# Hyena stages of a three-branch encoder: more tiles read ahead, another share of the merge, two vector steps on ScalarE

## Chip, core and metric

One NeuronCore of one Trainium2 chip runs the whole program. The metric is the device time of one execution in microseconds (us). Engines are named as the profile names them: PE (TensorE matmul), PEld (its weight load), DVE (VectorE), ACT (ScalarE), POOL (GpSimd), SP (SyncE, whose queue issues nearly all transfers).

## What is computed

An encoder layer runs on a prompt of 512 rows and a sample of 2048 rows, 1024 columns wide. A normalised row is projected by `w_in` (6672 columns) to three head groups: mLSTM (4 heads), retention (4 heads) and Hyena (512 channels). Their gated results are joined to 1536 columns, projected back by `w_out`, added to the input and normalised again.

```python
def hyena_branch(hy_in, hy_z, conv_w, conv_b, spec, skip):
    u = centred_conv3(hy_in, conv_w, conv_b)
    v, x1, x2 = u[..., :HY_WIDTH], u[..., HY_WIDTH:2*HY_WIDTH], u[..., 2*HY_WIDTH:]
    z = x1 * long_conv(v, spec[:, 0], skip[0])
    z = x2 * long_conv(z, spec[:, 1], skip[1])
    return z * silu(hy_z)
```

`long_conv` is a product in the frequency domain. Its filters come from a small network with two sines, `sin(freq * (x @ w + b))`, whose hidden values are multiplied by `w3` and a decaying window.

## The kernel before, in words

All matmuls with `w_in` are split in fp16 high and low parts, three products for each. `proj_T` (line 539, L544) gives transposed results, four groups of 6 matmuls of 512 columns; `proj_N` (line 549, L554) gives row-wise ones. The rows stand in five blocks of 512, block 0 the prompt.

The stages follow each other so:

- `front` (line 238): norm and transposition of the rows, the first third of Hyena's input with its 3-tap convolution (`hyena_cols`, `conv`, L811 and L813), the gates (`hyena_gate`), the filter network (`filter_mlp`, `sin`, L562 to L568), and the first set of filters.
- the merge (line 232): one stream is Hyena's Fourier work, the other the rest of Hyena's projections (`projections`) and then all of retention. The Hyena stream is `stage_a0` (L921: transform over n1 of the first third, from `X` to `Sg`), `freq(0)` (L948, L983: transform over n2, product with the filter, transform back to `Z`), `inv_a(0)` (L1028: back over n1, product with x1, and forward again by `stage_a`), `freq(1)`, and `inv_a(1)` (L1028, product with x2 at L1029, with the gate at L1033 on POOL, store to `ymix` at L1036).
- `mlstm`, then `final` (the product with `w_out`).

A stage over n1 takes 20 tiles (L, j): 4 of the prompt, 16 of the sample. In `inv_a(1)` a tile loads two `hb` buffers of `Z` (L890, 256 KB each), one of `X` and one of the gate `hyg` in two halves each (L790, 128 KB a half), and stores one in two halves (L1036): eight transfers. All of them, and those of the other stream, are issued in order on SP. There are 18 `hb` buffers.

The order of the work is planned when the program is built. Generators yield a cost in microseconds of PE work; `lag(cost, lag)` (line 172) adds the time before which the stream is not to be taken again. `merge` (line 177) takes, of the streams that are due, the one with the smallest share of its total done, cost so far divided by the number given with it: `275 * W3` = 283.25 for Hyena and 848 for the other. If no stream is due, the planned time jumps to the next due one. The framework (`schedule_with_timeline_sim=True`) then orders the instructions of each engine by its own estimate of what is ready, with the planned order as priority; so an instruction can pass an earlier one.

Two waits of the planner matter at the start of the merge. `filters()` in `projections` (line 290) begins with `lag(0.0, FH)`, 8 us. A Hyena projection of group 1 or 2 stops after its first 24 matmuls (`while grp and grp - 1 not in self.scaled`, line 828) until the filters of the group before are summed.

The end of the merge is the last block of the last retention head (`RtHead.second`, `output`, lines 1673 to 1709), which has no next block to be merged with. Its lags are R1 = 2.5, R2 = 2.0, R3 = 1.5, four times R4 = 0.6, and LN = 1.5, around 0.86 + 0.43 + 4 x 0.43 us of PE cost and 0.1.

Of the kernel before, what the change touches and what calls it, by code (L numbers as in the profile page):

```python
# [14 lines left out]
AF = mybir.ActivationFunctionType  # L15
ALU = mybir.AluOpType
# [14 lines left out]
MAGIC = 12582912.0  # L31
# [7 lines left out]
LF, LA, LI, LT, W1, W2, W3, LN, LM = 2.7, 1.0, 4.2, 1.6, 0.8, 1.08, 1.03, 1.5, 3.5  # L39
# [4 lines left out]
def geo(L):  # L44
    N = 2 * L
    N1 = N // 64
    V = N1 // 2
    return dict(N=N, N1=N1, K1=N1 // 2, V=V, GF=128 // N1, GS=128 // V, NTF=N // 128, NTS=L // 128)
# [105 lines left out]
class Trunk:  # L154
# [62 lines left out]
    def run(self):  # L217
        tc = self.tc
        with ExitStack() as ctx:
            self.psum = ctx.enter_context(tc.tile_pool(name="psum", bufs=8, space=PSUM))  # L220
            self.dram = ctx.enter_context(tc.tile_pool(name="dram", bufs=1, space=DRAM))
            self.cp = ctx.enter_context(tc.tile_pool(name="cp", bufs=1))
            self.setup()
            with ExitStack() as c1:
                self.hp = c1.enter_context(tc.tile_pool(name="hp", bufs=1))
                self.wp = c1.enter_context(tc.tile_pool(name="wp", bufs=2))
                self.hT = [[self.T(self.hp, [128, 8, 512], "h", F16, bufs=10) for i in range(2)] for b in range(5)]
                self.filter_pool = ExitStack()
                self.drain(self.front())
                with tc.tile_pool(name="hy", bufs=2, side="right") as self.hy:  # L230
                    self.load_ai()
                    self.drain(self.merge((self.chain(self.stage_a0(), self.freq(0), self.inv_a(0), self.freq(1), self.inv_a(1)), 275 * W3),
                                          (self.chain(self.projections(), self.retention()), 848)))
                self.drain(self.mlstm())
                with tc.tile_pool(name="fin", bufs=2, **TW) as self.fin:
                    self.final()
# [322 lines left out]
    def sin(self, pool, out_list, x, p):  # L559
        nc = self.nc  # L560
        k = self.T(pool, [128, 512], "sink")
        nc.vector.tensor_scalar(k[:p], x, 1.0 / (2 * math.pi), MAGIC, op0=ALU.mult, op1=ALU.add)  # L562
        nc.vector.tensor_scalar(k[:p], k[:p], MAGIC, None, op0=ALU.subtract)
        nc.vector.scalar_tensor_tensor(x, k[:p], -PI_C1, x, op0=ALU.mult, op1=ALU.add)
        nc.vector.scalar_tensor_tensor(x, k[:p], -PI_C2, x, op0=ALU.mult, op1=ALU.add)
        nc.vector.tensor_scalar(x, x, PI_MAX, -PI_MAX, op0=ALU.min, op1=ALU.max)
        for o, i in out_list:
            nc.scalar.activation(o, i, AF.Sin)  # L568
# [22 lines left out]
    def mlp_setup(self):  # L591
        nc, I, pm = self.nc, self.I, self.pm
        w1 = self.T(pm, [33, 64], "w1", bufs=1)
        w2 = self.T(pm, [64, 2, 64], "w2", bufs=1)
        pv = self.T(pm, [128, 3], "pv", bufs=1)
        nc.sync.dma_start(w1, I['hy_w1'][0])
        for i in range(2):
            nc.sync.dma_start(w2[:, i], I['hy_w2'][0])
            for j, nmv in enumerate(('hy_b1', 'hy_b2', 'hy_freq')):
                nc.sync.dma_start(pv[i * 64:(i + 1) * 64, j:j + 1], I[nmv].rearrange("o k -> k o"))  # L600
        self.fm = (w1, w2, pv)
        self.hid = [self.T(self.dram, [128, 512], f"hid{i}") for i in range(10)]

    def filter_blocks(self):
# [201 lines left out]
                    nc.gpsimd.tensor_copy(us[nb][:, 513 - end:514 - end], u[:, own:own + 1])  # L806
        return us, put

    def conv(self, d, u, w, bias):
        nc = self.nc  # L810
        nc.vector.tensor_scalar(d, u[:, 0:512], w(0), bias, op0=ALU.mult, op1=ALU.add)  # L811
        for t in (1, 2):
            nc.vector.scalar_tensor_tensor(d, u[:, t:t + 512], w(t), d, op0=ALU.mult, op1=ALU.add)  # L813

    def hyena_cols(self, grp, cp, cis, w):

        nc, hc = self.nc, self.hyc
        cv = {}
        halo = {ci: self.halo_blocks(hc, range(5), f"u{cis.index(ci)}") for ci in cis}

        def step(b):
            for ci in cis:
                us, put = halo[ci]
                c = grp * 4 + 2 * cp + ci
                ps = self.ps()
                yield from self.proj_T(ps, w, ci * 128, b)
                put(b, ps, w[2])
                while grp and grp - 1 not in self.scaled:
                    yield self.lag(0.0, 1.0)
                for d in (x for x in range(5) if (x == b and b in (0, 4)) or (x == b - 1 and b > 1)):  # L830
                    L = LP if d == 0 else LS
                    if d < 2:
                        cv[ci, L] = self.T(hc, [128, L], f"cv{L}", bufs=len(cis))
                    s, o = self.sw[L], d * 512 - SEQ0[L]
                    self.conv(cv[ci, L][:, o:o + 512], us[d], lambda t: s[:, t, c:c + 1], s[:, 3, c:c + 1])
                yield 1.28

        def out(L):
            nt = geo(L)['NTS']
            for ci in cis:  # L840
                cb = 2 * cp + ci
                for j0 in range(0, nt, 4):
                    ps = self.ps()
                    for jj in range(4):
                        j = j0 + jj
                        nc.tensor.transpose(ps[:, jj * 128:(jj + 1) * 128], cv[ci, L][:, j:L:nt], self.ident)  # L846
                    xs = self.T(hc, [128, 4, 128], "xs", bufs=3)
                    nc.scalar.activation(xs, ps.rearrange("p (j c) -> p j c", j=4), AF.Copy)
                    nc.sync.dma_start(self.X[grp][L][j0:j0 + 4, :, cb * 128:(cb + 1) * 128].rearrange("j p c -> p j c"), xs)
                    yield 0.43  # L850
        return step, out

    def hyena_proj(self, grp, *after):
# [42 lines left out]
    def stage_a0(self):  # L896
        seq = [(L, j) for L in (LP, LS) for j in range(geo(L)['NTS'])]
        st = {}

        def load(i):  # L900
            L, j = seq[i]
            st[i] = self.hx(0, L, j)

        n = len(seq)
        load(0)
        load(1)
        for i in range(n + 1):
            if i:
                L, j = seq[i - 1]
                self.stage_a(L, 0, j, st.pop(i - 1))  # L910
            if i + 2 < n:
                load(i + 2)
            yield self.lag(0.86, 1.5)

    def stage_a(self, L, o, j, t):
        nc = self.nc
# [92 lines left out]
    def inv_a(self, o):  # L1009
        nc = self.nc  # L1010
        seq = [(L, j) for L in ((LS, LP), (LP, LS))[o] for j in range(geo(L)['NTS'])]
        zs, xs, st = {}, {}, {}

        def load(i):
            L, j = seq[i]
            zs[i] = [self.hb(self.Z[L, o][:, geo(L)['NTS'] * h + j::2 * geo(L)['NTS'], :]) for h in range(2)]

        def load_x(i):
            L, j = seq[i]
            g = self.in_halves(self.half_rows(self.hyg, L, j)) if o == 1 else None  # L1020
            xs[i] = self.hx(o + 1, L, j), g

        def mid(i):
            L, j = seq[i]
            z, (x, g) = zs.pop(i), xs.pop(i)
            ps = self.ps()
            for h in range(2):
                nc.tensor.matmul(ps[64 * h:64 * h + 64], self.ai[L][:, 128:192], z[h], start=True, stop=True)  # L1028
            nc.vector.tensor_tensor(out=x, in0=x, in1=ps, op=ALU.mult)  # L1029
            if o == 0:  # L1030
                st[i] = x
            else:
                nc.gpsimd.tensor_tensor(out=g, in0=g, in1=x, op=ALU.mult)  # L1033
                rows = self.half_rows(self.ymix[:, 1024:1536], L, j)
                for h in range(2):
                    nc.sync.dma_start(rows[h], g[64 * h:64 * h + 64])  # L1036

        def back(i):
            L, j = seq[i]
            self.stage_a(L, 1, j, st.pop(i))  # L1040

        n = len(seq)
        load(0)
        yield self.lag(0.0, 5.0)
        for i in range(-1, n + 1):
            if o == 0 and i >= 1:
                back(i - 1)
            if 0 <= i < n:
                mid(i)
            if i + 1 < n:  # L1050
                load_x(i + 1)
            if i + 2 < n:
                load(i + 2)
            yield self.lag(1.71 if o == 0 else 0.86, LI)

    def gates(self):
        nc, I, tc = self.nc, self.I, self.tc
# [678 lines left out]
```

## Time and profile before

| | us |
|---|---|
| median of 3 runs | 2651.07 |
| the runs | 2650.94 to 2654.84 |
| the profiled execution, its own time | 2648.68 |
| its span, first to last instruction | 2646.9 |
| mean granted clock of TensorE, share of full speed | 0.988 |

The span is what the views of the trace divide. The profiled execution's own time is 1.8 us longer than its span, and 2.4 us below the median of the runs. "Idle before" names what an engine waited for just before an instruction. A wait for several things is put down to the one that came last.

### The profile page before, as it was taken

The page shows a single profiled execution, that of the slowest core. Times are in us where ns is not written, and L with a number is a line of the kernel's source. Part 1 is how long each engine was busy: PE and PEld are TensorE (multiplying, and loading weights), DVE is VectorE, ACT ScalarE, POOL GpSimd, SP SyncE. Part 2 cuts the span into 40 slices and gives each one's busy share as a digit, 9 for nine tenths or more (in the row PEclk, how much of TensorE's full clock was granted, in tenths as well). Part 3 has the DMA queues.
Part 4 walks back from the last instruction along what each step waited for, and adds up shares of the span by engine and source line. Part 5 has one row for each costly group of instructions (what it writes and reads, how often), then busy time and mean ns, then how long its engine had stood idle before and what let it go on. Part 6 is the DMA issues. An engine that isn't in the chain of part 4 may idle for free.

```text
span 2646.9 us, 45607 instructions
## 1 busy us (share of the span) xinstructions
PE 2557.2 (97%) x17830; PEld 1770.2 (67%) x17830; DVE 1338.3 (51%) x3070; ACT 1053.7 (40%) x2030; POOL 493.9 (19%) x647
## 2 busy tenths in 40 slices
PE   7999979999999999999999979999999999899998
PEld 5565543444446777777777747787887777788887
DVE  6875635665554434545444444565556645522222
ACT  6455646442233333423333323555445545411111
POOL 0103312331011122322232341111111111100000
PEclk9999989999999999999999989999999999999999
DMA  6233377564454665434333782222121322322331
GB/s 207 84 99 108 98 220 252 167 187 127 126 160 128 207 198 160 126 100 132 116 104 97 226 228 65 52 66 61 37 64 42 89 73 59 133 102 95 111 104 48
DMA packets 238049, 321.30 MB, mean 121 GB/s; under 512 B 22755, under 2 KB 125947, under 8 KB 237833
## 3 DMA queue, kind: packets, MB, share of 16 engines
q1 hardware_dynamic: 237752, 318.11, 39.8%
q8 instruction: 141, 2.31, 0.4%
q14 instruction: 76, 0.61, 0.1%
q0 software_dynamic: 80, 0.26, 0.0%
HBM read 205.41 MB, written 112.89 MB: 120 GB/s over the span
## 4 chain that ended last, share of the span: by engine, by line
PE 78%; DMA 6%; ACT 4%; DVE 4%; issue 1%; SPq 1%; POOL 1%; DVEq 0%; POOLq 0%; ACTq 0%
PE ps L554 27%; PE ps L544 13%; PE ps L1287 13%; PE ps L948 6%; DMA rb<-rowd 3%; PE ps L983 3%; PE ps L1028 2%; PE ps L921 1%; PE ps L1639 1%; DMA wraw<-in_w_in 1%; PE ps L693 1%; PE ps L1438 1%; PE ps L1275 1%; PE ps L1698 1%; PE ps L846 1%
## 5 line engine op out<-in xcount | busy, mean ns | idle before, releaser
L554 PE MATMUL ps<-whi,h 128*128 128x256 f16 (+2 forms) x6080 | 913.7, 256 | 0.0
L554 PEld LDWEIGHTS <-h 128*128 128x128 f16 x9120 | 776.0, 98 | 150.0 <-issue 69.5
L554 PE MATMUL ps<-wlo,h 128*128 128x256 f16 (+2 forms) x3040 | 734.6, 256 | 0.0
L544 PE MATMUL ps<-h,whi 128*128 128x512 f16 x1600 | 484.9, 383 | 4.0 <-ACT whi L526 4.0
L544 PE MATMUL ps<-h,wlo 128*128 128x512 f16 x800 | 305.0, 381 | 0.0
L544 PEld LDWEIGHTS <-whi 128*128 128x128 f16 x1600 | 151.1, 99 | 212.8 <-issue 63.0
L1287 PE MATMUL ps<-h,yh 128*128 128x512 f32 x760 | 210.6, 396 | 1.6 <-ACT yh L369 1.6
L948 PE MATMUL ps<-hb,cB 128*64 128x512 f32 x640 | 165.9, 605 | 0.2 <-DMA hb<-F 0.2
L1287 PEld LDWEIGHTS ps<-h,yh 128*128 128x128 f32 x760 | 141.6, 188 | 33.7 <-ACT yh L369 1.9
L668 POOL TENSOR_TENSOR acc<-acc,win 128x512 f32<-128x512 f32 x80 | 107.2, 1340 | 201.4 <-ACT win L667 196.2
L544 PEld LDWEIGHTS <-wlo 128*128 128x128 f16 x800 | 78.7, 98 | 94.7 <-issue 4.9
L1618 POOL TENSOR_TENSOR m<-raw,tb 128x256 f32<-128x256 f32 x80 | 72.3, 904 | 336.2 <-ACT raw L1615 273.2
L1287 PE MATMUL ps<-h,yl 128*128 128x512 f32 x380 | 120.9, 395 | 0.0
L1615 ACT ACTIVATE raw<-ps,winv 128x256 f32<-128x256 f32 x80 | 37.8, 473 | 167.5 <-PE ps L554 98.9
L662 DVE TENSOR_TENSOR f<-ps,win 128x512 f32<-128x512 f32 x80 | 55.0, 688 | 88.7 <-PE ps L378 66.1
L813 DVE SCALAR_TENSOR_TENSOR cv<-u,sw,cv 128x512 f32<-128x512 f32 x120 | 98.1, 838 | 1.1
L527 DVE SCALAR_TENSOR_TENSOR wlo<-wraw,wsc,whi 128x512 f16<-128x512 f32 (+2 forms) x116 | 82.6, 749 | 22.8 <-ACT whi L526 21.6
L1637 ACT ACTIVATE vw<-va,rtv 128x128 f32<-128x128 f32 x144 | 51.9, 398 | 100.4 <-PE ps L1639 100.0
L948 PEld LDWEIGHTS ps<-hb,cB 128*64 128x64 f32 x640 | 41.5, 136 | 73.2 <-issue 60.6
L348 DVE TENSOR_REDUCE wam<-wraw 128x1 f32<-128x2048 f32 (+2 forms) x29 | 60.0, 2069 | 60.0 <-DMA wraw<-in_w_in 60.0
L1343 DVE TENSOR_TENSOR xt<-xt,ps 128x512 f32<-128x512 f32 x40 | 25.8, 684 | 126.9 <-PE ps L1287 126.9
L971 POOL TENSOR_TENSOR hb<-hb,hb 128x512 f32<-128x512 f32 x40 | 50.9, 1273 | 185.5 <-DVE hb L970 176.3
(318 smaller groups left out, 4045.8 us busy)
## 6 DMA issues: line engine op xcount, KB each, us to landing
F<-fo SPq DMA_DIRECT2D x160, 128.0 KB, 2.4
Sg<-hb SPq DMA_DIRECT2D x80, 256.0 KB, 2.3
hb<-F SPq DMA_DIRECT2D x80, 256.0 KB, 4.3
hb<-Sg SPq DMA_DIRECT2D x80, 256.0 KB, 5.1
Z<-hb SPq DMA_DIRECT2D x80, 256.0 KB, 3.5
hb<-Z SPq DMA_DIRECT2D x80, 256.0 KB, 3.7
rb<-rowd SPq DMA_DIRECT2D x80, 256.0 KB, 5.1
wraw<-in_w_in SPq DMA_DIRECT2D x36, 512.0 KB, 5.8
```

The lines of the kernel that those rows point to most:

```text
L348: self.nc.vector.tensor_reduce(am[:, 0:1], src, axis=AX.XY if len(src.shape) == 3 else AX.X, op=ALU.max, apply_absolute_value=True)
L527: v = nc.vector.scalar_tensor_tensor(lo[:, k], raw[:, k], s, hi[:, k], op0=ALU.mult, op1=ALU.subtract)
L544: nc.tensor.matmul(out, w[x][:, k, wc:wc + 128], self.hT[b][y][:, k], start=(k == 0 and i == 0), stop=(k == 7 and i == 2))
L554: nc.tensor.matmul(out, self.hT[b][x][:, k, c * 128:(c + 1) * 128], w[y][:, k, wc:wc + n], start=(k == 0 and i == 0), stop=(k == 7 and i = ...
L662: nc.vector.tensor_tensor(out=f, in0=ps, in1=win, op=ALU.mult)
L668: nc.gpsimd.tensor_tensor(out=acc, in0=acc, in1=win, op=ALU.add)
L813: nc.vector.scalar_tensor_tensor(d, u[:, t:t + 512], w(t), d, op0=ALU.mult, op1=ALU.add)
L948: nc.tensor.matmul(ps[half[h]], Cs[i][:, 128 * h + 64 * r:128 * h + 64 * r + 64], src[h], start=True, stop=True)
L983: nc.tensor.matmul(pz[h], c[half[h], 256 + 128 * r:384 + 128 * r], y[r][half[h]], start=(r == 0), stop=(r == 1))
L1028: nc.tensor.matmul(ps[64 * h:64 * h + 64], self.ai[L][:, 128:192], z[h], start=True, stop=True)
L1287: self.nc.tensor.matmul(self.pss[n], a[p], w[q][:, n * 512:(n + 1) * 512], start=(k == 0 and i == 0), stop=(k == 11 and i == 2))
L1618: nc.gpsimd.tensor_tensor(out=m, in0=raw[:, :, ::-1], in1=sin[:, c:c + 2], op=ALU.mult)
```

## The change

Six edits: (1) Hyena's total in the merge goes from 275 to 295 times W3, 303.85. (2) `stage_a0` loads four tiles ahead in place of two; it then waits 9 planned us, and yields cost 1.0 and lag 0.5 per tile in place of 0.86 and 1.5. (3) `inv_a` loads tiles 0 and 1 whole (Z, X and gate) and waits 7 planned us. Each turn now does `mid`, then the loads of the tile two ahead, then `back` of the tile before; X and gate were loaded one tile ahead, and `back` came first. (4) A turn of `inv_a` yields cost 2.0 (order 0) or 1.0 (order 1) and lag 1.5, in place of 1.71 or 0.86 and lag LI = 4.2. (5) The first tap of the convolution of Hyena's group 0 is an ACT instruction (Identity with scale and bias by partition), 20 of them. (6) The first step of the sine, x/2pi + MAGIC, is an ACT instruction, 20 of them, with one memset for its bias.

```diff
-self.drain(self.merge((self.chain(self.stage_a0(), ... self.inv_a(1)), 275 * W3),
+self.drain(self.merge((self.chain(self.stage_a0(), ... self.inv_a(1)), 295 * W3),
...
-        nc.vector.tensor_scalar(k[:p], x, 1.0 / (2 * math.pi), MAGIC, op0=ALU.mult, op1=ALU.add)
+        nc.scalar.activation(k[:p], x, AF.Identity, bias=self.magic[:p], scale=1.0 / (2 * math.pi))
...
+        self.magic = self.T(pm, [128, 1], "magic", bufs=1)
+        nc.vector.memset(self.magic, MAGIC)
...
-    def conv(self, d, u, w, bias):
+    def conv(self, d, u, w, bias, scalar=False):
...
+        if scalar:
+            nc.scalar.activation(d, u[:, 0:512], AF.Identity, bias=bias, scale=w(0))
+        else:
+            nc.vector.tensor_scalar(d, u[:, 0:512], w(0), bias, op0=ALU.mult, op1=ALU.add)
...
-                    self.conv(..., s[:, 3, c:c + 1])
+                    self.conv(..., s[:, 3, c:c + 1], grp == 0)
... stage_a0
-        load(0)
-        load(1)
-        for i in range(n + 1):
-            if i:
-                L, j = seq[i - 1]
-                self.stage_a(L, 0, j, st.pop(i - 1))
-            if i + 2 < n:
-                load(i + 2)
-            yield self.lag(0.86, 1.5)
+        for i in range(4):
+            load(i)
+        yield self.lag(0.0, 9.0)
+        for i in range(n):
+            L, j = seq[i]
+            self.stage_a(L, 0, j, st.pop(i))
+            if i + 4 < n:
+                load(i + 4)
+            yield self.lag(1.0, 0.5)
... inv_a
-        load(0)
-        yield self.lag(0.0, 5.0)
-        for i in range(-1, n + 1):
+        for i in range(2):
+            load(i)
+            load_x(i)
+        yield self.lag(0.0, 7.0)
+        for i in range(n + 1):
+            if i < n:
+                mid(i)
+            if i + 2 < n:
+                load(i + 2)
+                load_x(i + 2)
             if o == 0 and i >= 1:
                 back(i - 1)
-            if 0 <= i < n:
-                mid(i)
-            if i + 1 < n:
-                load_x(i + 1)
-            if i + 2 < n:
-                load(i + 2)
-            yield self.lag(1.71 if o == 0 else 0.86, LI)
+            yield self.lag(1.0 if o else 2.0, 1.5)
```

## Rows read from the trace of the kernel before

**Rows 1.** The page, part 1: busy time and share of the span.

```profile
PE 2557.2 (97%) x17830; PEld 1770.2 (67%) x17830; DVE 1338.3 (51%) x3070; ACT 1053.7 (40%) x2030; POOL 493.9 (19%) x647
```

**Rows 2.** Busy time by stretch: PE, PEld, DVE, ACT, POOL; clock, DMA share, GB/s.

```profile
1545.00:1595.00 50.00, 34.59 (x143) 15.26 (x142) 19.94 (x51) 5.73 (x13) 18.43 (x24) 0.83 0.67 190
...
410.00:1545.00 1135.00, 1131.09 (x7871) 708.67 (x7869) 555.69 (x1236) 415.93 (x853) 288.56 (x316) 1.00 0.51 155
1600.00:2250.00 650.00, 634.27 (x5676) 502.69 (x5677) 377.50 (x1083) 328.76 (x657) 84.13 (x164) 0.99 0.24 60
355.00:390.00 35.00, 22.75 (x90) 8.92 (x88) 11.04 (x17) 12.12 (x21) 2.02 (x4) 0.82 0.79 246
1475.00:1545.00 70.00, 70.00 (x557) 54.28 (x556) 35.90 (x80) 23.32 (x58) 33.08 (x28) 1.00 0.87 251
```

**Rows 3.** What PE waited for, 1545 to 1600 us: total, times, longest.

```profile
PE ps L1028 <- DMA hb<-Z: 11.1, 3, 4.8
```

**Rows 4.** Line L1028 alone by stretch: PE, PEld, clock, DMA share, GB/s.

```profile
1475.00:1545.00 70.00, 12.94 (x44) 2.36 (x44) 1.00 0.87 251
1545.00:1595.00 50.00, 16.51 (x32) 2.90 (x32) 0.83 0.67 190
```

**Rows 5.** PE in order of time, the end of the merge: start, us.

```profile
1577.06 3.44 PE L1028 MATMUL ps<-hb,ai 128*64 128x512 f32 x4 [4.80 <-DMA hb<-Z]
...
1585.44 1.04 PE L544 MATMUL ps<-h,whi 128*128 128x512 f16 x2
...
1591.11 1.07 PE L1028 MATMUL ps<-hb,ai 128*64 128x512 f32 x2
```

**Rows 6.** The chain that ended last: L544 at half and at full clock.

```profile
623.88 3.88 PE ps L544 x18
...
1585.51 5.67 PE ps L544 x17
```

**Rows 7.** SP in order of time: five tiles of `inv_a(1)`, first to last.

```profile
1479.76 1.06 SPq L890 DMA_DIRECT2D hb<-Z  x2
...
1482.11 1.18 SPq L1036 DMA_DIRECT2D ymix<-hb  x2
1483.38 1.18 SPq L790 DMA_DIRECT2D hb<-X  x2
...
1504.91 1.00 SPq L890 DMA_DIRECT2D hb<-Z  x2
```

**Rows 8.** SP and PE in order of time, entry to `inv_a(1)`.

```profile
1465.15 1.05 SPq L890 DMA_DIRECT2D hb<-Z  x2
...
1460.62 1.13 PE L983 MATMUL ps<-hb,cB 64*128 64x512 f32 x4
```

**Rows 9.** The page, part 6: size, median us from issue to landing.

```profile
hb<-Z SPq DMA_DIRECT2D x80, 256.0 KB, 3.7
```

**Rows 10.** All engines in order of time, start of the merge.

```profile
362.64 0.83 SPq L779 DMA_DIRECT2D ai<-c_AI  x2
...
363.51 3.81 SPq L790 DMA_DIRECT2D hb<-X  x6
...
367.07 3.78 PE L921 MATMUL ps<-hb,ai 64*128 64x512 f32 x8 [8.14 <-DMA hb<-X]
```

**Rows 11.** What PE waited for, 330 to 410 us.

```profile
PE ps L376 <- ACT w L369: 4.1, 1, 4.1
```

**Rows 12.** Groups by line, the front (0 to 352 us): count, busy us, mean ns.

```profile
L656 ACT ACTIVATE win<-dl,tneg 128x512 f32<-128x512 f32 x40 | 28.7, 720 | 29.6 <-POOL acc L668 27.6 <-POOL u L803 2.0
...
L811 DVE TENSOR_SCALAR cv<-u,sw 128x512 f32<-128x512 f32 x20 | 11.7, 583 | 11.6 <-ACT u L800 11.6
...
L562 DVE TENSOR_SCALAR sink<-sx 64x512 f32<-64x512 f32 (+1 forms) x20 | 8.2, 415 | 0.1
```

**Rows 13.** What PE waited for, 0 to 200 us.

```profile
PE ps L738 <- ACT h L568: 3.2, 1, 3.2
PE ps L440 <- DVE xt L434: 2.8, 2, 2.2
```

More of the change, by code (lines that the diff above doesn't have):

```diff
@@ L231, in run @@
                     self.load_ai()
-                    self.drain(self.merge((self.chain(self.stage_a0(), self.freq(0), self.inv_a(0), self.freq(1), self.inv_a(1)), 275 * W3),
+                    self.drain(self.merge((self.chain(self.stage_a0(), self.freq(0), self.inv_a(0), self.freq(1), self.inv_a(1)), 295 * W3),
                                           (self.chain(self.projections(), self.retention()), 848)))
@@ L807, in halo_blocks @@
         return us, put
-    def conv(self, d, u, w, bias):
+    def conv(self, d, u, w, bias, scalar=False):
         nc = self.nc
-        nc.vector.tensor_scalar(d, u[:, 0:512], w(0), bias, op0=ALU.mult, op1=ALU.add)
+        if scalar:
+            nc.scalar.activation(d, u[:, 0:512], AF.Identity, bias=bias, scale=w(0))
+        else:
+            nc.vector.tensor_scalar(d, u[:, 0:512], w(0), bias, op0=ALU.mult, op1=ALU.add)
         for t in (1, 2):
@@ L834, in step @@
                     s, o = self.sw[L], d * 512 - SEQ0[L]
-                    self.conv(cv[ci, L][:, o:o + 512], us[d], lambda t: s[:, t, c:c + 1], s[:, 3, c:c + 1])
+                    self.conv(cv[ci, L][:, o:o + 512], us[d], lambda t: s[:, t, c:c + 1], s[:, 3, c:c + 1], grp == 0)
                 yield 1.28
```

## The prediction

> **What bounds the kernel now.** I read the busy shares first, then the busy time by stretch, then the waits of PE in the stretches with gaps, then SP's order in time. PE is busy in 97% of the span [rows 1]. So only a stretch where PE stands idle, or runs at a lower clock, can give anything back. The stretches [rows 2] show where the merge has such room. From 410 to 1545 us PE is busy 1131.09 of 1135, 3.9 us idle. From 355 to 390 it is busy 22.75 of 35, at a mean clock of 0.82. From 1545 to 1595 it is busy 34.59 of 50, at 0.83. So the merge loses at its two ends, not in between.
>
> The late end is the Hyena stream's tail. In the last 55 us L1028 waited for its Z loads three times, 11.1 us [rows 3]. Retention's matmuls had ended, and nothing else stood in front of those tiles. The tail costs 50 - 34.59 = 15.4 us of idle time. The clock costs more: L1028 took 12.94 us for 44 instructions before the tail, 0.294 each, and 16.51 for 32 in it, where 9.4 would do [rows 4]: 7.1 us. And 17 L544 took 5.67 us where 18 take 3.88 at full clock [rows 6]: 2.0. All told 24.5 us.
>
> Why Hyena is last follows from the planner. Before `inv_a(1)` its costs are 18.1 + 102.6 + 37.6 + 102.6 = 260.9 of 283.25, 92% of its share (freq: 1.71 x 60). A tile of `inv_a(1)` then can't come sooner than 0.86 + 4.2 = 5.06 planned us after the one before. Twenty take over 101. Less than that is left of the other stream.
>
> **The change, part by part.** *Share and lags of inv_a(1).* The new costs before it are 20 + 102.6 + 42 + 102.6 = 267.2 of 303.85, 88%. So freq(1) ends about 4% of the merge earlier, near 1410 us in place of 1462. A tile at its share now takes 1.0 + 848/303.85 = 3.79 planned us. Twenty take 76, and the stage would end some 60 planned us before retention. The tail's 24.5 us then go, as long as something else is paid for less:
>
> (a) Retention's last block stands alone. Its lags and costs sum to 2.5 + 0.86 + 2.0 + 0.43 + 1.5 + 4 x (0.43 + 0.6) + 1.5 + 0.1 = 13.0 planned us, 3.1 of it PE work. Upper bound 9.9 us idle. Lower bound 0: the first mLSTM matmuls can run ahead, as they do here, at 1585.44, before the last L1028 at 1591.11 [rows 5]. I take 4, the idle time of one head in mLSTM, which has no Hyena beside it: (650 - 634.27)/4 [rows 2]. The 60 us of retention without Hyena add 1.5 at that stretch's 2.4%. Together 5.5.
>
> (b) The transfers can't follow 3.79 us. From 1479.76 to 1504.91 SP issues five tiles without a pause, eight transfers each, 5.03 us a tile with the other stream's loads between them [rows 7]. The bytes give the same: 1.31 MB a tile (5 x 256 KB) at the 251 GB/s of this stretch [rows 2] are 5.2 us. Nineteen steps at 5.03 are 95.6 us, against 72 planned, or about 65 if the stage makes up the arrears of its opening wait at 2.5 to 3 us a tile. Two tiles are loaded ahead, 6 issues of 0.55 each, 6.6 us. Upper bound 95.6 - 65 - 6.6 = 24 us of waiting in L1028. Retention's matmuls stand behind it on PE and its own stores behind on SP. Lower bound 0: the instruction order isn't the planned one, and at 1585.44 [rows 5] L544 was put between two halves of one tile, so work can be moved in front of a late Z. From 1475 to 1545 PE was busy 70.00 of 70 us [rows 2] and waited for none, but at 6 us a tile. I take 10, a little under the middle, as that row is the nearer one.
>
> (c) Entry. From the end of L983, 1460.62 + 1.13, to the issue of Z, 1465.15 [rows 8], and 3.7 us to land [rows 9] are 7.1 us; the new wait is 7, the old ones were 5.0 + 5.06. Bounds 0 and 3 for each `inv_a`; I take 0.5 each.
>
> *Order in inv_a(0).* A turn issues the same six transfers. Its share is 2.0 x 3.79 = 7.6 us a tile, above the 3.3 us that SP needs. Moving `back` behind `mid` gives L1029 a turn more. Nothing, hidden by the 3.9 us of slack of that stretch.
>
> *Start of the merge.* PE stood 8.14 us at 358.9 for the first X tile [rows 10]: SP could issue `ai` at 362.64 and X at 363.51 only, when the front's buffers were free. Reading four tiles ahead issues them at the same moment. The wait of 9 planned us gives PE nothing to do before, since the projection stops after 24 matmuls and the filters wait their own 8. So the stall stays. Bounds -8.1 and +2.2: two more X tiles, four issues, stand on SP ahead of the w3 load for which PE waited 4.1 us [rows 11]. I take +1.
>
> *Front.* Twenty taps leave DVE, 583 ns each, and twenty sine steps, 415 [rows 12]. ACT gets forty instructions. The nearest row is L656, one operand per partition, same shape, 720 ns. DVE loses 11.7 + 8.2 = 19.9 us, ACT gains 28.8. PE waited 2.8 us on DVE and 3.2 on ACT's sine chain here [rows 13]. The first can go, the second can double: bounds -2.8 and +3.2, taken as 0. All else runs beside PE, and would cost its 28.8 us only if ACT were late for every matmul.
>
> I count no activation table load for Identity: L1203 uses that function already.
>
> The Trainium skill speaks against these two moves: "ScalarE: Activation LUTs", Rules for kernel authors, puts multiply and add on VectorE, not ScalarE. The rows agree on the price, 720 ns against 583 and 415. By that rule, with the difference on the path, the sum would be higher by the 8.9 us that the fifth case below works out.
>
> **Sum.** -24.5 + 5.5 + 10 + 1 + 1 + 0 = -7.0 us. On the profiled execution that is 2648.7 - 7.0 = 2641.7; on the median of 2651.07, 2.4 above it, 2644.1. About 0.2%, 5.3 us, can be told from no change here.
>
> **The rivals.** *Forecast, 0.40:* as summed, 2644. For it: the tail's waits are real and nothing needs that order. Against: it lives on (b).
>
> *Start too, 0.10:* the first X wait goes with the lag, 8 more, 2636. Against it: SP's order [rows 10].
>
> *Cancelled, 0.20:* (b) at 17 in place of 10: 2651. That is about where the gain ends.
>
> *Slower, 0.25:* the tail's waits move into the stage. One mechanism: SP and the transfers give a tile each 5.03 us, PE keeps the planned order, and L1028 waits in each of some 18 tiles. Price: 24 us of waiting, and 7.1 for a clock that falls as it did in the tail [rows 4]. -24.5 + 5.5 + 31.1 + 1 + 1 = +14.1, 2665. It decides from 17 us of waiting on. For it: PE did wait at just these loads where it had nothing else [rows 3]. Against it: the halves that were split.
>
> *ACT in the front, 0.05:* the two steps lengthen the chains, 20 x (720 - 583) + 20 x (720 - 415) ns = 8.9 us. 2644.1 + 8.9 = 2653, no change.
>
> **Numbers.** The predicted time is the forecast's, 2644. Its own range is 2636 to 2650. The whole range, 2629 to 2664, takes in the start's bound with (b) at half below, and the slower case's middle above; about 1 in 10 is left out on each side. Faster by over 0.2%: 0.40 + 0.10. Within it: 0.20 + 0.05. Slower: 0.25.
>
> **What would show it.** Right: the last L1028 lies 40 us or more before retention's last matmul, and the stretch after it has no wait on Z; PE is idle under 6 us between retention's end and mLSTM's L544. (b) is read from PE's waits at L1028 on Z: 10 us expected, 17 turn the sign. The first L921 still waits about 8 us. In the front DVE shows 20 us less, ACT 29 more, and PE's busy time by stretch is as before. Wrong: L1028 waits in most tiles of `inv_a(1)`, or the tail is still last.

## The result, and the profile after

The changed kernel takes 2682.7 us (median of 4 runs, 2678.7 to 2683.5) against 2651.0 for the kernel before beside it (4 runs): a ratio of 1.0115, 95% interval 1.0097 to 1.0132. It is 32 us slower where 7 us less was forecast, and outside the range. In the code after the change L921 is L926, L948 is L953, L983 is L988, L1028 is L1033, L1036 is L1041.

The page of the profiled execution after, part 1 (busy time of each engine), answers to [rows 1]:

```profile
PE 2574.5 (96%) x17830; PEld 1772.8 (66%) x17830; DVE 1315.4 (49%) x3031; ACT 1082.7 (40%) x2070; POOL 488.4 (18%) x647
```

The span grew from 2646.9 to 2680.5 us. PE has the same 17830 instructions, but is busy 17.3 us longer, and idle 16.3 us longer. Both halves need a cause. Busy time by stretch of the kernel after, columns as in [rows 2]:

```profile
410.00:1437.00 1027.00, 1022.11 (x6971) 620.98 (x6970) 504.32 (x1106) 378.79 (x763) 241.35 (x276) 1.00 0.49 151
1437.00:1553.00 116.00, 94.88 (x495) 51.16 (x492) 31.98 (x77) 15.99 (x42) 36.56 (x32) 0.88 0.77 219
1553.00:1590.00 37.00, 37.00 (x334) 34.09 (x334) 18.28 (x50) 14.42 (x34) 14.00 (x14) 1.00 0.11 32
1590.00:1629.10 39.10, 31.38 (x272) 25.52 (x270) 18.85 (x57) 11.35 (x28) 11.11 (x19) 0.90 0.20 51
1629.10:1676.60 47.50, 46.24 (x403) 33.09 (x404) 23.90 (x52) 16.19 (x27) 5.55 (x9) 0.94 0.34 82
```

The damage is in one place. From 1437 to 1553 us, the stage `inv_a(1)`, PE is idle 21.1 us and its clock is 0.88; the same stage before lost nothing until its tail [rows 2]. The second loss is smaller: 7.7 us idle between 1590 and 1629, the bare end of retention. What PE waited for from 1380 to 1680 us (total, times, longest) names the first:

```profile
PE ps L1033 <- DMA hb<-Z: 18.7, 7, 3.9
PE ps L1416 <- ACT kT L1405: 2.8, 1, 2.8
PE ps L1033 <- DVE qN L1627: 2.4, 1, 2.4
```

The groups by line in the same window show what the waits do not. A tile is two matmuls, one for each half of its PSUM tile, and each of these f32 matmuls shows as two records, so the 20 tiles are 80 records. They took this (busy us, mean ns | idle before):

```profile
L1033 PE MATMUL ps<-hb,ai 128*64 128x512 f32 x80 | 44.1, 682 | 21.1 <-DMA hb<-Z 18.7 <-DVE qN L1627 2.4
```

That is 0.55 us a record. Before the tail of the kernel before it was 0.29 [rows 4]. One could put that down to the clock. PE in order of time, at a tile of the kernel before:

```profile
1489.75 1.08 PE L1028 MATMUL ps<-hb,ai 128*64 128x512 f32 x4
1490.76 0.28 PE L554 MATMUL ps<-whi,h 128*128 128x256 f16 x1
```

and in the kernel after:

```profile
1450.52 2.70 PE L1033 MATMUL ps<-hb,ai 128*64 128x512 f32 x4 [2.43 <-DVE qN L1627]
1456.85 1.94 PE L1033 MATMUL ps<-hb,ai 128*64 128x512 f32 x2 [3.63 <-DMA hb<-Z]
1458.72 0.39 PE L554 MATMUL ps<-whi,h 128*128 128x256 f16 x1
...
1465.21 1.07 PE L1033 MATMUL ps<-hb,ai 128*64 128x512 f32 x2
1466.22 0.39 PE L554 MATMUL ps<-whi,h 128*128 128x256 f16 x2
1466.45 0.27 PE L554 MATMUL ps<-wlo,h 128*128 128x256 f16 x1
1466.56 0.38 PE L554 MATMUL ps<-whi,h 128*128 128x256 f16 x2
1466.87 1.07 PE L1033 MATMUL ps<-hb,ai 128*64 128x512 f32 x2
...
1496.69 1.04 PE L1033 MATMUL ps<-hb,ai 128*64 128x512 f32 x2 [2.09 <-DMA hb<-Z]
1497.66 0.49 PE L1645 MATMUL ps<-vw,kN 128*128 128x128 f32 x2
1498.08 1.07 PE L1033 MATMUL ps<-hb,ai 128*64 128x512 f32 x2
```

In the kernel before all four records of a tile (x4) take 1.08 us. Here a half alone (x2) takes 1.07 us, 1.94 behind a wait (the granted clock is 0.54 from 1450 to 1460 us, near its lower level, 1.2 GHz), and the tile's other half takes its own 1.07 again. Five matmuls stand between the halves at 1465 and 1467, one between those at 1497 and 1498. In PE's order 15 of the 20 tiles have 1 to 27 other matmuls between their halves, 5 have none. So two mechanisms were to be told apart, halves run apart and a lower clock, and two causes of the waits: PE's order, and SP's. On SP, the waits of its queue from 1425 to 1545 us:

```profile
SPq L1041 <- POOL hb L1038: 19.8, 11, 4.6
```

The store of a finished tile stands on SP in front of the loads two tiles on, and waits there for GpSimd.

### The profile page after: what moved, and what is told of

It reads as the page before. It is cut to its first block, busy times and chain, and to the rows that moved or that the text cites. A ratio compares the mean times of both kernels' runs of the same rounds, so it can differ in the third digit from the quotient of the medians.

```text
span 2680.5 us, 45597 instructions
## 1 busy us (share of the span) xinstructions
PE 2574.5 (96%) x17830; PEld 1772.8 (66%) x17830; DVE 1315.4 (49%) x3031; ACT 1082.7 (40%) x2070; POOL 488.4 (18%) x647
## 4 chain that ended last, share of the span: by engine, by line
PE 40%; DMA 5%; DVE 3%; ACT 2%; issue 1%; SPq 1%; POOL 1%; DVEq 0%; POOLq 0%; ACTq 0%
PE ps L554 14%; PE ps L1293 12%; PE ps L544 4%; DMA rb<-rowd 3%; PE ps L1033 1%; DMA wraw<-in_w_in 1%; PE ps L1444 1%; DMA hb<-Z 1%; PE ps L1281 1%; PE ps L1516 1%; PE ps L953 1%; ACT y L1209 1%; DVE t L1472 1%; PE ps L1540 1%; PE ps L1543 1%
## 5 line engine op out<-in xcount | busy, mean ns | idle before, releaser
L544 PE MATMUL ps<-h,whi 128*128 128x512 f16 x1600 | 485.0, 383 | 3.2 <-ACT whi L526 3.2
L544 PE MATMUL ps<-h,wlo 128*128 128x512 f16 x800 | 304.4, 381 | 0.0
L544 PEld LDWEIGHTS <-whi 128*128 128x128 f16 x1600 | 150.5, 99 | 214.6 <-issue 68.1
L953 PE MATMUL ps<-hb,cB 128*64 128x512 f32 x640 | 163.8, 606 | 1.6 <-DMA hb<-F 1.6
L544 PEld LDWEIGHTS <-wlo 128*128 128x128 f16 x800 | 78.6, 98 | 94.8 <-issue 5.0
L818 DVE SCALAR_TENSOR_TENSOR cv<-u,sw,cv 128x512 f32<-128x512 f32 x120 | 92.2, 785 | 15.9 <-ACT cv L814 14.4
L953 PEld LDWEIGHTS ps<-hb,cB 128*64 128x64 f32 x640 | 40.6, 136 | 71.4 <-issue 56.3
L1033 PE MATMUL ps<-hb,ai 128*64 128x512 f32 x160 | 66.3, 650 | 21.1 <-DMA hb<-Z 18.7
```

What stands on the lines that cost most here:

```text
L544: nc.tensor.matmul(out, w[x][:, k, wc:wc + 128], self.hT[b][y][:, k], start=(k == 0 and i == 0), stop=(k == 7 and i == 2))
L953: nc.tensor.matmul(ps[half[h]], Cs[i][:, 128 * h + 64 * r:128 * h + 64 * r + 64], src[h], start=True, stop=True)
```

## The experiments

Each ratio is to the kernel before, run beside it on the same chip; its median there was 2647 to 2651 us. Differences in us to other kernels are between medians taken at different times, and can be off by these 4 us.

**The step of `inv_a(1)` alone set back** (`e1_wide_lag`, on the kernel after):

```
-            yield self.lag(1.0 if o else 2.0, 1.5)
+            yield self.lag(1.0, 4.2) if o else self.lag(2.0, 1.5)
```

> The changed kernel, with the step of inv_a(1) alone set back to 5.2 planned us a tile (1.0 + 4.2 in place of 1.0 + 1.5). Its PE order has 18 to 52 other matmuls before each tile where the changed kernel has 0 to 48, about 20 on the mean. Theory 'pace' (PE's order packs tiles at 3.8 us, transfers give one in 5 or more, and the idle PE loses its clock): L1033 waits for Z under 3 us in inv_a(1), the 80 L1033 of the stage take 24 us and not 44, the stage ends before retention; 2625 to 2640 us. Rival 'bare end' (retention without Hyena beside it is what costs): the last 60 us stay as in the changed kernel, 2665 or more. Rival 'read-ahead' (loading both Z and X two tiles ahead is what jams SP): waits of 10 us or more stay, 2660 or more.

Measured: 2631.1 us, 0.9934 (0.9916 to 0.9952), 51.6 less than the kernel after, and the lowest median here. The stage by stretch, and its line:

```profile
1437.00:1553.00 116.00, 114.65 (x923) 88.65 (x921) 60.45 (x140) 34.06 (x84) 55.20 (x48) 1.00 0.80 241
```

```profile
L1033 PE MATMUL ps<-hb,ai 128*64 128x512 f32 x80 | 21.6, 618 | 0.0
```

The first L1033 of the stage starts at 1433.8 and the last at 1553.9 us; in the kernel after it is 1432.3 and 1552.8. The hurried stage takes as long as the wide one, but from 1437 to 1553 us PE gets through 495 matmuls, the stage's own among them, where with the wide step it gets through 923. No wait on Z is left, and all 20 tiles are whole. The mean rate of the transfers is higher here, 241 GB/s against 219, so the 21 us of waits were not the most that they can carry. Of the rivals, the read-ahead and the bare end fall: both are still in this kernel.

**Loads three tiles ahead and in front of the stores** (`e2_three_ahead`, on the kernel after):

```
-        for i in range(2):
+        for i in range(2 + o):
...
+            if o == 1 and i + 3 < n:
+                load(i + 3)
+                load_x(i + 3)
             if i < n:
                 mid(i)
-            if i + 2 < n:
+            if o == 0 and i + 2 < n:
```

> The changed kernel, but inv_a(1) loads three tiles ahead, and issues them ahead of the tile's two ymix stores on SP. Theory 'pace': the transfers still give a tile in 5 us or more and PE's order still packs them, so L1033 waits for Z 12 us or more, 2672 to 2690 us. Rival 'loop' (Z of tile i+2 stands on SP behind the store of tile i, which waited 23.6 us for GpSimd; the loop from load to store sets the pace): the waits fall under 5 us, the clock comes back, 2635 to 2650.

Measured: 2664.6 us, 1.0056 (1.0035 to 1.0078), 18 less than the kernel after and between the two theories. SP's wait for GpSimd in the same window, and PE's wait on Z:

```profile
SPq L1041 <- POOL hb L1038: 6.4, 2, 5.9
```

```profile
PE ps L1033 <- DMA hb<-Z: 11.5, 5, 3.5
```

SP's wait fell from 19.8 us, so the loop over SP was part of it, but 11.5 us of waits and 40.0 us of L1033 remain.

**The same without the gate loads** (`e7_three_no_gate_load`; six transfers a tile, the gate left out of `ymix`):

```
-            g = self.in_halves(self.half_rows(self.hyg, L, j)) if o == 1 else None
...
-                nc.gpsimd.tensor_tensor(out=g, in0=g, in1=x, op=ALU.mult)
+                nc.gpsimd.tensor_tensor(out=x, in0=x, in1=x, op=ALU.mult)
```

> The kernel of three tiles ahead (11.5 us of waits, 2664.6 us) without the loads of the gate tiles in inv_a(1): GpSimd squares the product instead, so the gate is left out of ymix. Six transfers and 1.05 MB a tile in place of eight and 1.31. Theory 'transfers' (what is left in that kernel is the rate of the transfers, 5.2 us a tile against PE's 3.8): a tile in 4.2 us, waits under 4 us, L1033 of the stage 24 to 30 us in place of 40, 2640 to 2652 us. Rival 'order' (PE's bunches, two or three tiles with few matmuls between them, cost the clock and the waits whatever the rate): 2658 to 2668.

Measured: 2644.0 us, 0.9987 (0.9978 to 0.9997). The stage by stretch, and its line (L1032 here):

```profile
1437.00:1515.00 78.00, 78.00 (x474) 45.32 (x472) 31.90 (x73) 15.31 (x40) 29.91 (x30) 1.00 0.82 246
```

```profile
L1032 PE MATMUL ps<-hb,ai 128*64 128x512 f32 x80 | 35.5, 617 | 0.0
```

All waits are gone and the tiles come every 4.4 us (1428.7 to 1512.7, 19 steps), against 5.6 with the gate (1431.9 to 1537.9). So what was left of the waits hangs on the gate's loads. Whether it is their number, their bytes or the buffers that they hold, this run does not say, as all three fell (three `hb` a tile in place of four). And L1032 still takes 35.5 us, with the clock at 1.00 and no wait: the clock is not what makes it long. Of the expectation on L1033, 24 to 30, this part was missed.

**The halves kept together** (`e9_after_paired`, on the kernel after):

```
-            for h in range(2):
-                nc.tensor.matmul(ps[64 * h:64 * h + 64], ...)
+            for h in (1, 0):
+                m = nc.tensor.matmul(ps[64 * h:64 * h + 64], ...)
+                if h == 0:
+                    self.tc.keep_in_program_order(m)
```

> The changed kernel with the two half-tile matmuls of each inv_a(1) tile kept next to each other in PE's order (second half's matmul first, the other pinned behind it). In the traces so far two halves side by side take 1.08 us together, a half that stands alone takes 1.07 by itself; the changed kernel has 31 rows of halves alone. Theory 'halves' (L1033's 44 us against 21.6 with the wide step are halves run apart, not the lower clock): L1033 of the stage 22 to 27 us. Rival 'clock' (they are long because the granted clock fell): 38 us or more. For the time: if waits and halves add up, 18 us less, 2658 to 2668; if the transfers set the length of the stage all the same ('pace'), the waits on Z grow from 18.7 us by what the halves give back, and the time stays within 8 us of 2680.

Measured: 2666.1 us, 1.0068 (1.0048 to 1.0089), 16.6 less than the kernel after. L1033 of the stage, its waits, and the stage by stretch:

```profile
L1033 PE MATMUL ps<-hb,ai 128*64 128x512 f32 x80 | 26.1, 732 | 23.0 <-DMA hb<-Z 22.9
```

```profile
1437.00:1553.00 116.00, 89.13 (x590) 58.84 (x589) 36.07 (x89) 18.85 (x49) 42.25 (x37) 0.87 0.76 227
```

All 20 tiles are whole, the clock is as low as before at 0.87, and L1033 takes 18.0 us less, where 15 split tiles by 1.06 us make 15.9. This is the run that decides: 44.1 - 26.1 = 18.0 us are halves apart. The 4.5 us from 26.1 to the wide kernel's 21.6 go with the clock: 15 tiles take 1.08 us, and five behind a wait of 2.7 us or more take 1.97 or 1.98, the first of them where the granted clock is 0.52 (1450 to 1460 us). The waits rose by 4.2 us only.

**Halves pulled apart where nothing waits** (`e10_wide_split`, on the wide step):

```
                 nc.tensor.matmul(ps[64 * h:64 * h + 64], ...)
+                if o == 1 and h == 0:
+                    yield self.lag(0.5, 0.5)
...
+            yield self.lag(0.5, 3.7) if o else self.lag(2.0, 1.5)
```

> The kernel with the wide step (2631 us, no waits on Z, every tile's halves side by side), with a step of the planner between the two halves of a tile: the same 5.2 planned us a tile, the order now puts other matmuls between the halves in at least 15 of 20 tiles. Theory 'halves': 1.0 us more for each of 15 to 20 tiles, L1033 of the stage 36 to 43 us in place of 21.6, granted clock 1.00 and no wait on Z, 2645 to 2653 us. Rival 'clock' (halves apart cost nothing as long as PE is kept busy): 2629 to 2635.

Measured: 2640.3 us, 0.9971 (0.9962 to 0.9981), 9.3 more than the wide step. Its line in the stage, and two halves in order of time:

```profile
L1033 PE MATMUL ps<-hb,ai 128*64 128x512 f32 x80 | 37.6, 618 | 0.0
```

```profile
1484.40 1.07 PE L1033 MATMUL ps<-hb,ai 128*64 128x512 f32 x2
1485.41 0.28 PE L554 MATMUL ps<-whi,h 128*128 128x256 f16 x1
...
1486.82 1.07 PE L1033 MATMUL ps<-hb,ai 128*64 128x512 f32 x2
```

The line grew by 16.0 us, as expected, with the clock at 1.00 and no wait on Z. Of it the time shows 9.3. PE's whole busy time grew by 11.3 (2551.5 to 2562.8), its idle time fell by 2.5; the other 4.7 us are spread over many lines, at most 1.0 us in one, and the mean granted clock of this execution was 0.991 against 0.989. The clock alone as a cause is refuted, the time's growth was expected 5 to 13 us too high.

**Both mends** (`e11_three_paired`: the edits of the runs with three tiles ahead and with the halves together).

> Both mends in one: three tiles ahead with the loads in front of the stores, and the halves kept side by side. With three tiles ahead alone: 11.5 us of waits, 40 us of L1033, 2664.6 us. If the two costs add up: waits as there, L1033 22 to 27 us, 2645 to 2652. Theory 'pace' (a tile comes in 5.2 us whatever PE does): the waits on Z rise to 20 us or more and the time stays at 2658 to 2668.

Measured: 2663.1 us, 1.0058 (1.0036 to 1.0079): no better than three tiles ahead alone. L1033 fell from 40.0 to 25.2 us, the waits on Z rose from 11.5 to 19.8:

```profile
PE ps L1033 <- DMA hb<-Z: 19.8, 9, 7.0
```

Here the transfers set the pace, 5.4 us a tile (1431.1 to 1532.9), and what PE saves it waits. SP issues the eight transfers of a tile, from one store to the next, without a pause in 5.04 us:

```profile
1441.25 1.18 SPq L1043 DMA_DIRECT2D ymix<-hb  x2
...
1446.29 1.18 SPq L1043 DMA_DIRECT2D ymix<-hb  x2
```

From 1431 to 1533 us the mean rate is 256 GB/s. Mending PE and SP did not help the stage here, as PE's order runs through it at under 4 us a tile; the wide step did.

**The parts alone, on the kernel before.** The new `inv_a` alone, at share 275:

> The kernel before with the new inv_a alone (order, read-ahead, lags), share 275. Theory 'pace': the same bunched order, 15 to 20 us of waits on Z and about 20 us of clock, against the 24.5 us of the tail: 2660 to 2680 us. Rival 'share' (the stage hurts only because it comes 40 us earlier and leaves retention bare): no slower than before, 2638 to 2652.

Measured: 2676.6 us, 1.0105 (1.0087 to 1.0124). PE's waits on Z over the whole run, and the stage's line:

```profile
PE ps L1028 <- DMA hb<-Z: 13.6, 8, 3.8
```

```profile
L1028 PE MATMUL ps<-hb,ai 128*64 128x512 f32 x80 | 42.1, 628 | 13.6 <-DMA hb<-Z 13.6
```

The share is not needed for the damage. The share alone (`275 * W3` to `295 * W3`):

> The kernel before with share 295 in place of 275 and nothing else: inv_a(1) keeps its 5.06 planned us a tile. Theory 'pace': tiles at 5.06 wait for nothing and the tail goes, its 24.5 us less 10 to 15 for a bare end of retention: 2635 to 2643 us. Rival 'bare end' (what retention loses without Hyena is as much as the tail): 2647 to 2652. Rival 'share' (the larger share alone makes the waits): 2665 or more.

Measured: 2641.6 us, 0.9974 (0.9961 to 0.9987). The larger share by itself is a gain: the tail goes, with 3.2 us of waits on Z left. The start alone (the new `stage_a0`):

> The kernel before with the new stage_a0 alone (four X tiles ahead, one wait of 9 planned us, cost 1.0). The prediction's term: +1, within -8.1 and +2.2, so 2649 to 2652 us, and the first L921 after its 8 us wait as before. Rival 'start gains': the wait at the first X goes, 2642 to 2645.

Measured: 2657.1 us, 1.0038 (1.0028 to 1.0049), outside what was expected. The first L921 came at 369.6 us against 367.1, but this lay there before the edit could act: a load of `hd` in the front is issued at 210.25 us where the kernel before has 207.38. The last L948, in freq(1), came at 1461.1 against 1442.5. The Hyena stream ran 18.6 us later, some 3 of them from there, and its tail waited longer, 15.6 us where [rows 3] has 11.1. From 1545 us to the first matmul of mLSTM it is 63.7 us, where it was 55.7; that is 8.0 of the 8.3 us by which the span grew:

```profile
PE ps L1028 <- DMA hb<-Z: 15.6, 4, 4.5
```

Whether it costs anything where there is no tail was tried with the old `stage_a0` in the kernel with the wide step:

> The kernel with the wide step and share 295 (2631 us), with the stage_a0 of the kernel before: two X tiles ahead, a step of 0.86 + 1.5. Alone, the new stage_a0 cost 10 us, with the Hyena stream 18 us later at the end of freq(1) and a longer tail. Theory 'tail' (the start costs through that tail alone, which is not there at share 295): within 3 us of 2631. Theory 'start' (it costs PE time where it stands): 8 to 10 less, 2621 to 2624.

Measured: 2633.8 us, 0.9959 (0.9947 to 0.9972), where the wide step with the new start has 0.9934 (0.9916 to 0.9952). No cost of the start shows there, and the 8 to 10 us less that were expected of a cost in itself did not come. So its cost is through the tail, as far as these two runs show.

The front's two moves alone, then the sine's and the tap's:

> The kernel before with the two moves to ScalarE in the front alone. Theory 'front gains' (first L926 at 361.3 in place of 367.1 us): 4 to 6 us less, 2645 to 2647. Rival 'start gains' (it is the four tiles read ahead that bring that): no change, 2650 to 2652. By the chain of 8.9 us counted in the prediction: 2656 to 2660.

> The kernel before with the first step of the sine alone on ScalarE (20 instructions). The two moves together gave 11 us. Theory 'sine' (the sine's five steps on VectorE are the chain that the filters wait for): 6 to 11 us less, 2639 to 2644. Theory 'conv' (the taps are what VectorE is late with): 0 to 3 less, 2646 to 2650. By the prediction's lengthened chain: 6 us more.

> The kernel before with the first convolution tap of the front alone on ScalarE (20 instructions). Theory 'conv': 6 to 11 us less, 2639 to 2644. Theory 'sine': 0 to 3 less, 2646 to 2650. If each gives what it takes off VectorE (11.7 and 8.2 us), at the rate of both (11 of 19.9): 6 us here, 5 with the sine.

Measured: both 2639.0 us, 0.9959 (0.9944 to 0.9973), 11 us less where 4 to 6 were expected; the sine 2643.5, 0.9991 (0.9981 to 1.0001), which can't be told from nothing; the tap 2637.9, 0.9967 (0.9956 to 0.9978). The tap is the gain. The front's groups with the tap alone moved, the first tap on ScalarE and the two others on VectorE:

```profile
L816 DVE SCALAR_TENSOR_TENSOR cv<-u,sw,cv 128x512 f32<-128x512 f32 x40 | 32.8, 827 | 14.2 <-ACT cv L812 13.7 <-POOL u L806 0.3
...
L812 ACT ACTIVATE cv<-u,sw 128x512 f32<-128x512 f32 x20 | 16.2, 811 | 0.6
```

and the two others in the kernel before:

```profile
L813 DVE SCALAR_TENSOR_TENSOR cv<-u,sw,cv 128x512 f32<-128x512 f32 x40 | 38.1, 968 | 0.1
```

VectorE loses the tap's 11.7 us [rows 12] and 5.3 more, as the other taps take 827 ns for 968. The start of the merge with the tap alone, in order of time:

```profile
355.60 3.81 SPq L790 DMA_DIRECT2D hb<-X  x6
...
358.84 4.03 PE L924 MATMUL ps<-hb,ai 64*128 64x512 f32 x8 [9.29 <-DMA hb<-X]
```

X is issued at 355.60 in place of 363.51 [rows 10], 7.9 us earlier, and that is most of the 9. PE still waits for it. But the lead is older than the merge: the load of `hd` at 207.38 us in the kernel before is issued at 202.28 here, 5.1 us earlier. What PE waited for from 95 to 160 us, and the busy time from 120 to 140 (columns as in [rows 2]), in the kernel before:

```profile
PE ps L440 <- DVE xt L434: 2.2, 1, 2.2
...
120.00:140.00 20.00, 17.84 (x68) 7.40 (x67) 14.40 (x25) 6.25 (x12) 4.67 (x8) 0.83 0.23 80
```

and with the tap alone moved:

```profile
PE ps L440 <- DVE xt L434: 0.5, 1, 0.5
...
120.00:140.00 20.00, 19.52 (x110) 10.88 (x109) 17.99 (x33) 11.27 (x20) 4.43 (x10) 1.00 0.23 81
```

The wait for VectorE goes, and with it the lower clock behind it (0.50 from 130 to 135 us before). The three other runs without the front's moves show the same as the kernel before, a wait of 2.2 to 2.4 us, 0.83 and 68 matmuls; all others have 0.5 to 0.9 us, 0.91 to 1.00 and 86 to 110. The sine alone relieves this stretch as well (0.6 us, 1.00, 110 matmuls), but has X only 2.6 us earlier; why it keeps less was not traced, nor was the rest of the tap's 7.9 us.

**A share between** (`e8_wide_287`, the wide step at 287) **and the gains without the rest** (`e12_front_share`: front, share 295 and halves together on the kernel before).

> The kernel with the step of 5.2 planned us, with share 287 in place of 295. Its order has the last L1033 14 matmuls before retention's last, where share 295 has it 52 before. Theory 'bare end' (10 us of idle time between 1550 and 1600 us in the kernel at share 295 are retention alone, and Hyena's last tiles can fill them): 2620 to 2627 us. Rival (those waits stay whatever lies beside them, or the tail comes back): 2629 to 2636.

> A kernel of the parts that gained: the front's two moves and share 295, with the lags, the order and the start of the kernel before, and the halves kept side by side. If the parts add up (front -11, share -7): 2628 to 2634 us. If the share's gain is the same slack that the front's gain has used: 2636 to 2641.

Measured: 2642.0 us, 0.9978 (0.9962 to 0.9993), and 2639.9, 0.9969 (0.9954 to 0.9984). The share of 287 lost, outside both expectations: PE is idle 5.7 of the 10 us from 1560 to 1570, and 4.0 of the 20 from 1580 to 1600. Hyena's last tiles do not fill the end of retention. The front's gain and the share's do not add up either: 0.41 and 0.26% alone, 0.31 together.

## Why the prediction was wrong

*The tail, -24.5.* That it would go was right: the last L1033 starts at 1552.8 us, 65 us before retention's last L1708 at 1617.9, and nothing waits on Z after it. Its working was not: 7.1 us were put down to the clock from [rows 4]. In that tail three of the eight tiles ran as halves apart. Two at full clock cost 1.07 + 1.07 - 1.08 = 1.06 us each; the third shows 1.94 and 1.07. That is some 3 us of the 7.1. And the tail was worth less than its sum. The share alone takes most of it away: L1028 fell from 52.1 to 45.2 us busy in the whole kernel, and its waits on Z from 11.1 to 3.2. Yet the time fell by 0.26%, some 7 us, where -24.5 + 5.5 would be -19. Part of the gain came back as cost in other lines: 4.4 us more idle before L948, 4.4 more busy in L983, 4.1 more idle before L1410.

*(b), +10 in 0 to 24. This is the step that failed.* It measured 21.1 us of idle time at L1033, 18.7 on Z: past the 17 from which it "decides", and inside the bound. What stands nowhere in the sum is the other price of the hurried order, 18.0 us of halves run apart and 4.5 us of clock at L1033. The choice near the lower end rested on a row misread: "at 1585.44 [rows 5] L544 was put between two halves of one tile, so work can be moved in front of a late Z". The work between two halves of a tile was the price itself: it takes apart two matmuls that run together, and costs a microsecond a tile. The chance to see it was there, as [rows 5] shows a half alone at 1591.11 with x2 and 1.07 us, and a whole tile is x4 in 1.08.

The row of 1475 to 1545 with PE busy all the time, taken as the nearer one, spoke of tiles at 6 us. The changed order gives PE under 4 us of work a tile, and that is what counted. The 5.03 us a tile from [rows 7] was near: 5.4 and 5.6 us with three tiles ahead. With two ahead it was 6.3 (1432.3 to 1552.8 over 19 steps), as the store waits on SP in front of the loads.

*The slower rival, 0.25,* had the place and the mechanism, with 7 waits on Z, not some 18. It gave 2665: 24 of waiting and 7.1 of clock. With the halves kept together the kernel takes 2666.1, with 22.9 us of waits and 4.5 of clock at L1033. The missing 17 us are the halves. That its total fits so closely is partly luck, as its sum holds neither the front's gain nor the tail's smaller worth.

*(a), 5.5.* The bare end shows 7.7 us idle and a clock of 0.90 from 1590 to 1629. From mLSTM's first L1416 to its first L1545 it took 47.5 us, where it was 42.7 before (1600.7 to 1643.4), at a clock of 0.94. So the term was too small. But the length of the bare stretch costs little: without the gate loads the stage ends 41 us earlier than with the wide step, and that kernel is 13 us slower. Its halves apart, 35.5 - 21.6 = 13.9 us of L1032, are the likeliest cause; that they are all of it is not shown, as in the split run 16.0 us of them gave 9.3 of time.

*(c), +1.* From the last L988 to the stage's first L1033 it is 9.2 us (1423.1 to 1432.3); before it was 10.0 (1461.2 to 1471.2). Right within a microsecond or two.

*Start, +1 in -8.1 to +2.2.* The wait at the first L926 stayed, 7.3 us, as said, though for `ai` in place of X. But alone the part cost 10 us, through a later Hyena stream and a longer tail, a path that the term did not have. At share 295 there is no such tail.

*Front, 0 in -2.8 to +3.2.* Minus 11 alone, and outside the bounds. VectorE is busy 22.9 us less over the span and ScalarE 29.0 more, near the 19.9 and 28.8 counted, at 811 ns a tap on ScalarE where 720 was taken. The term had the right wait, 2.8 us on VectorE [rows 13], and held that it can go. But it priced the wait alone, and not the lower clock behind it, which the same prediction did price in the tail. That the whole front, and with it the issue of X [rows 10], then comes earlier was not in the term either. The rule of the Trainium skill ("ScalarE: Activation LUTs", Rules for kernel authors), multiply and add on VectorE, is right on the price (811 against 583 ns), but here the slower engine had room and PE waited for the faster one: the tap on ScalarE gained 9 us.

*The parts* measured alone add up to -0.41 + 0.38 - 0.26 + 1.05 = +0.76%, the whole is +1.15%. With the share on top the stage does worse than with `inv_a` alone (44.1 us of L1033 and 18.7 of waits, against 42.1 and 13.6); the other 3 us of the difference were not traced.

*The span, by lines.* L1028 was busy 52.1 us and stood idle 11.1 before; L1033 after it 66.3 and 21.1. That is 24.2 of the 33.6 us by which the span grew. mLSTM's L1410, now L1416, waits 5.2 us more (6.5 to 11.7); the rest is spread over many lines and was not traced.

## What to carry to other kernels

A planned step below what a stage's transfers give did not shorten the stage here. It took the other stream's work away from beside it; set the step at the measured pace, here 5.2 for 5 to 6 us. Read the two matmuls of one PSUM tile as one unit, and look at whether a new order keeps them next to each other. Where a short wait on PE has a lower clock behind it, count both prices, in the front as in the tail.

## What was not expected of the hardware

Two f32 matmuls of 64 output columns, 128 x 512, on the two halves of one PSUM tile take 1.08 us together when nothing stands between them in PE's order, and about 1.07 each when a single other matmul does (1496.69 to 1498.08). PE did not pull the second half forward over it. That the array's parts can work at the same time agrees with the Trainium skill ("TensorEngine Tiling (Array Packing)", Key Properties), where independent tiles of the array may run matmuls in parallel.

On VectorE, the second and third taps got faster, 968 to 827 ns, when the first left the engine for ScalarE; no run here shows why.
